# Attention rows transposed three tiles behind their scores, weighted values one step later, with more row buffers

## The chip, the cores and the metric

The kernel runs on one core of one Trainium2 chip. The metric is device time in microseconds, from one launch to the end of the program, as the median of several runs. TensorE does the matrix products and the transposes, VectorE (DVE in the profile) and ScalarE (ACT) the work on rows, GpSimd (POOL) a few copies and masks, and SyncE (SP) issues most transfers.

## The reference

One decoder layer on 1024 tokens of width 1024, in float32. After an RMS norm one projection feeds three kinds of heads; their results go through one output projection, and a squared-ReLU MLP (width 4096) follows. The change touches the two kinds of attention:

```python
# stick-breaking, 6 heads of 64, strictly causal
z = einsum('bhqd,bhsd->bhqs', qi, k) * scale
log_1mb = where(mask, log_sigmoid(-z), 0.0)
tail = cumsum(log_1mb, axis=3, reverse=True) - log_1mb
A = where(mask, exp(log_sigmoid(z) + tail), 0.0)
o = einsum('bhqs,bhsd->bhqd', A, v)
# forgetting, 6 heads of 64, causal; c is the running sum of log forget gates
s = einsum('bhqd,bhsd->bhqs', qi, k) * scale + (c[q] - c[s])
o = einsum('bhqs,bhsd->bhqd', softmax(where(mask, s, -1e30)), v)
```

Two further units, `hg0` and `hg1`, are HGRN2 (a gated linear recurrence) and are computed by levels and chunks.

## The kernel before, in words

The mixing part is eight units, run in the order m0, hg0, m1, m2, m3, hg1, m4, m5. A unit m*p* is one stick-breaking head (h = 0) and one forgetting head (h = 1). Each unit has two parts. Its projection (`proj_attn`, or `proj_hg`) multiplies the normed input by the unit's weights; every product is made of three matmuls of rounded high and low parts (`mm3`, L167 to L169, output `pj`). Its core (`attn`) is the attention itself. The core of one unit is interleaved in the source with the projection of the next (`place`, with `SPAN` and `POW`); the core of the last unit, m5, is interleaved with the first part of the output projection (`wo_tile`, output `po`, the same three lines). The framework then schedules every engine's instructions from this source order with a planner of its own, and each engine runs its list strictly in that order. So between the score matmuls of a head and its transposes TensorE has projection matmuls to do, as far as they have not been used up: the text calls them filler.

A core works on 16 row tiles of 128 queries, in steps. A step s does three things:

- `qprep` (every second tile): queries transposed (`qtp`, L366), scaled into `qj` by ScalarE (L368) and VectorE (L369).
- `qtile`, tile s: the scores `z` on TensorE (L391, L392, mask L394), up to two pieces of at most 512 keys. For h = 0 VectorE scales them into a row tile `sbz` (L400), ScalarE takes exp and ln (L401, L402, tile `sbe`), VectorE scans (L404, tile `sbr`) and subtracts (L407), ScalarE takes exp (L408). For h = 1 VectorE subtracts the gates and takes the maximum (L413, tile `fxa`), ScalarE takes exp with a row sum (L425), VectorE the reciprocal, and ScalarE scales (L434).
- `back`, tile s - SKEW: TensorE transposes the finished row tile in blocks of 128 by 128 (`atp`, L446), and ScalarE (L450) or VectorE (L452) copies the result out of PSUM into `at`. Once a group of two tiles of both heads is through, `av` multiplies by the values (L465), in the same step, and the result is split into high and low parts.

Tiles have fixed numbers of buffers (`BUFS`): row tiles `zs` (these are `sbz`, `fxa`, and also the level tiles `hx` of HGRN2 and the squares of both norms), function tiles `e`, scan tiles `r`, and `at`. In PSUM the scores and the query transposes share three buffers, the row transposes have two, and `av` shares one with the key transposes `ktp` (L314).

## Time and profile before

| what | value |
|---|---|
| median of 3 runs | 1349.1 us (1346.22 to 1351.35) |
| the profiled execution's own time | 1347.27 us |
| its span, first to last instruction | 1345.5 us |
| mean granted TensorE clock | 0.977 |
| 0 to 70 us (norm, first projection) | PE busy 52.06 us, DVE 49.78, ACT 40.49 |
| 70 to 660 us (the eight cores) | PE busy 560.66 us, DVE 440.87, ACT 389.40 |
| 660 to 735 us (output projection, second norm) | PE busy 68.12 us, DVE 64.10, ACT 41.50 |
| 735 to 1345.5 us (MLP) | PE busy 602.18 us, DVE 431.03, ACT 255.63 |

PE is TensorE's matmuls and PEld its weight loads. A matmul's row runs to its modelled end, and the next one starts earlier: dense matmuls overlap in the table, so the busy time of PE overstates its work. What a matmul costs in a dense stretch is read from the distance of two starts. Each weighted-value product is two matmuls in the trace.

### The profile page before, as it was taken

How to read it: one execution, taken by the hardware profiler on the slowest of the kernel's cores; microseconds unless marked ns; L12 is line 12 of the kernel's file. 1: busy time of each engine (PE TensorE's matmuls, PEld its weight loads, DVE VectorE, ACT ScalarE, POOL GpSimd, SP SyncE). 2: the span in 40 equal slices, each digit the busy share in tenths (PEclk: the TensorE clock that was granted, in tenths of full speed). 3: DMA queues.
4: the chain of work that ended last, by engine and by line, in shares of the span. 5: the costliest groups of instructions: out<-in, count | busy, mean ns of one | idle time of the engine just before them, and what ended most of it. 6: DMA issues, size and time to landing. Idle time of an engine off the chain costs nothing.

```text
span 1345.5 us, 19762 instructions
## 1 busy us (share of the span) xinstructions
PE 1283.0 (95%) x7200; PEld 1063.1 (79%) x7200; DVE 985.8 (73%) x1844; ACT 727.0 (54%) x1557; POOL 90.3 (7%) x138
## 2 busy tenths in 40 slices
PE   4999889989999999999798999999999999999998
PEld 4978789878688988767586888888887788888887
DVE  6758798766768788867579766666666897786965
ACT  5658445877878457776446454455454433333330
POOL 7000021002110130000000000000000000000000
PEclk9999999989899989999898999999999999999999
DMA  8200220301203025524443434444445972634322
GB/s 231 46 17 18 62 58 18 92 16 54 49 17 79 17 57 177 183 64 125 149 152 107 164 126 164 164 130 145 149 163 175 391 247 94 218 96 153 113 79 94
DMA packets 129737, 156.57 MB, mean 116 GB/s; under 512 B 46684, under 2 KB 73308, under 8 KB 129640
## 3 DMA queue, kind: packets, MB, share of 16 engines
q1 hardware_dynamic: 104496, 109.14, 26.8%
q10 hardware_dynamic: 25144, 46.17, 9.6%
q8 instruction: 57, 0.93, 0.3%
q14 instruction: 40, 0.33, 0.1%
HBM read 108.07 MB, written 47.21 MB: 115 GB/s over the span
## 4 chain that ended last, share of the span: by engine, by line
PE 80%; DVE 10%; ACT 4%; DMA 4%; issue 2%; SPq 0%; ACTq 0%; DVEq 0%
PE pj L167 6%; PE pj L169 6%; PE pj L168 6%; PE av L465 3%; PE atp L446 2%; PE pc L1021 2%; PE pc L1022 2%; PE pc L1023 2%; PE pd L1021 2%; PE pd L1022 2%; PE pd L1023 2%; PE pc L1202 2%; PE pc L1200 2%; PE pc L1201 2%; PE pa L1023 2%; PE pa L1021 2%
## 5 line engine op out<-in xcount | busy, mean ns | idle before, releaser
L167 PE MATMUL pj<-whi,hTh 128*128 128x384 f32 (+2 forms) x512 | 172.2, 339 | 0.0
L169 PE MATMUL pj<-whi,hTl 128*128 128x384 f32 (+2 forms) x512 | 171.9, 336 | 0.0
L168 PE MATMUL pj<-wlo,hTh 128*128 128x384 f32 (+2 forms) x512 | 170.6, 334 | 0.5 <-DVE wlo L127 0.4
L124 ACT CAST fah<-ya 128x1024 fp32r<-128x1024 f32 x56 | 58.7, 1048 | 166.8 <-PE pd L1201 50.0
L167 PEld LDWEIGHTS pj<-whi,hTh 128*128 128x128 f32 x512 | 98.7, 193 | 3.6 <-issue 1.1
L168 PEld LDWEIGHTS pj<-wlo,hTh 128*128 128x128 f32 x512 | 98.5, 192 | 3.5 <-issue 1.3
L169 PEld LDWEIGHTS pj<-whi,hTl 128*128 128x128 f32 x512 | 98.4, 192 | 2.3 <-issue 1.5
L127 DVE TENSOR_TENSOR fal<-ya,fah 128x1024 fp32r<-128x1024 f32 x56 | 68.3, 1219 | 23.2 <-ACT fah L124 23.1
L465 PE MATMUL av<-at,vst 128*64 128x256 f32 x480 | 71.3, 384 | 6.3 <-DVE at L452 3.0
L450 ACT COPY at<-atp 128x128 f32<-128x128 f32 (+3 forms) x120 | 55.5, 475 | 20.5 <-PE atp L446 19.5
L465 PEld LDWEIGHTS av<-at,vst 128*64 128x64 f32 x480 | 38.3, 144 | 33.2 <-issue 8.4
L127 DVE TENSOR_TENSOR fbl<-w2raw,fbh 128x1024 fp32r<-128x1024 f32 x48 | 58.0, 1215 | 1.6 <-ACT fbh L124 1.6
L408 ACT ACTIVATE sbz<-sbz 128x128 f32<-128x128 f32 (+3 forms) x72 | 37.7, 525 | 37.8 <-DVE sbz L407 37.2
L400 DVE TENSOR_SCALAR sbz<-z,qnr 128x128 f32<-128x128 f32 (+3 forms) x72 | 42.5, 611 | 20.6 <-PE z L394 12.9
L167 PE MATMUL po<-woh,mTh 128*128 128x512 f32 x128 | 52.1, 409 | 4.5 <-DMA mTh<-mix_m 3.6
L124 ACT CAST fbh<-w2raw 128x1024 fp32r<-128x1024 f32 x48 | 50.0, 1047 | 8.1 <-DMA w2raw<-in_w_ff_dram 5.1
L391 PE MATMUL z<-kst,qj 128*128 128x512 f32 (+3 forms) x144 | 51.3, 384 | 2.8 <-ACT qj L368 2.8
L1201 PE MATMUL pa<-fbl,fah 128*128 128x512 f32 x128 | 50.3, 395 | 1.9 <-DVE fbl L127 1.8
L1200 PE MATMUL pd<-fbh,fah 128*128 128x512 f32 x128 | 49.5, 399 | 2.3 <-ACT fbh L124 2.3
L168 PE MATMUL po<-wol,mTh 128*128 128x512 f32 x128 | 51.1, 399 | 0.0
L392 PE MATMUL z<-kst,qj 128*128 128x512 f32 (+3 forms) x144 | 49.6, 370 | 1.5 <-DVE qj L369 1.4
L169 PE MATMUL po<-woh,mTl 128*128 128x512 f32 x128 | 50.6, 398 | 0.0
(349 smaller groups left out, 3626.3 us busy)
## 6 DMA issues: line engine op xcount, KB each, us to landing
w1raw<-in_w_ff_dram SPq DMA_DIRECT2D x32, 512.0 KB, 4.6
w2raw<-in_w_ff_dram SPq DMA_DIRECT2D x16, 1024.0 KB, 7.1
ya<-yd_s SPq DMA_DIRECT2D x32, 512.0 KB, 3.6
yd_s<-y ACTq DMA_DIRECT2D x48, 256.0 KB, 4.6
ya<-yd_a SPq DMA_DIRECT2D x24, 512.0 KB, 3.7
wraw<-in_w_in_dram SPq DMA_DIRECT2D x48, 192.0 KB, 3.0
mix_m<-ot ACTq DMA_DIRECT2D x10, 512.0 KB, 3.7
wraw<-in_w_in_dram SPq DMA_DIRECT2D x16, 256.0 KB, 3.6
```

The lines of the kernel that those rows point to most:

```text
L124: S.copy(hi, raw)
L127: lo_eng.tensor_tensor(out=lo, in0=raw, in1=hi, op=ALU.subtract)
L167: PE.matmul(o, lhsT=lh, rhs=rh, start=start, stop=False)
L168: PE.matmul(o, lhsT=lh, rhs=rl, start=False, stop=False)
L169: PE.matmul(o, lhsT=ll, rhs=rh, start=False, stop=stop)
L450: S.copy(dst, tv)
L465: PE.matmul(o[h * HD:(h + 1) * HD, c0:], lhsT=st["v"][j // 4][:, j % 4, h, :], rhs=at[h][j // 4][:, j % 4, c0:], start=(j == 0), stop=(j = ...
L1021: PE.matmul(o, lhsT=wh[:, k], rhs=bh[:, k], start=start and k == 0, stop=False, **kw)
L1022: PE.matmul(o, lhsT=wh[:, k], rhs=bl[:, k], start=False, stop=False, **kw)
L1023: PE.matmul(o, lhsT=wl[:, k], rhs=bh[:, k], start=False, stop=k == 3, **kw)
L1200: PE.matmul(o, lhsT=lh[:, ts], rhs=rh, start=start and q == q0, stop=False, **kw)
L1201: PE.matmul(o, lhsT=lh[:, ts], rhs=rl, start=False, stop=False, **kw)
```

## The change

The transposes come three tiles behind the scores, not two. `av` is no longer called at the end of `back`, but at the next step, behind that step's scores and ahead of its transposes; the last group's follows its transposes at once. There are three more row tiles `zs` (8), one more function tile `e` (3) and one more scan tile `r` (3). Room for them (6144 of the 10240 bytes a partition) comes from the scratch area for dynamic DMAs; a padding tile of the MLP's second half grows by the same 6144 bytes, so that later tiles keep their places.

```diff
-    "BUFS": {... "zs": 5, "e": 2, "r": 2, ...},
+    "BUFS": {... "zs": 8, "e": 3, "r": 3, ...},
-    "SKEW": [2, 2, 2, 2, 2, 2],
+    "SKEW": [3, 3, 3, 3, 3, 3],
...
                 if cur["n", g] == 2:
-                    av(g)
+                    ready.append(g)
...
         steps = []
+        ready = []
...
                 if s < len(tiles):
                     qtile(*tiles[s])
+                while ready:
+                    av(ready.pop())
                 if s >= SKEW:
                     back(*tiles[s - SKEW])
+                if s == len(tiles) + SKEW - 1:
+                    av(ready.pop())
...
-    PLACES = {"f_m": {... "pad": (1, [P, 136 + 2048])},
+    PLACES = {"f_m": {... "pad": (1, [P, 136 + 3584])},
...
-    nc = _bacc.Bacc("TRN2", ..., dynamic_dma_scratch_size=8192)
+    nc = _bacc.Bacc("TRN2", ..., dynamic_dma_scratch_size=2048)
```

The planner makes a new order of the whole mixing part. Three places of TensorE's list show it. The first is the end of m0's core, where the last stick-breaking row tiles (`sbz`) are transposed; before:

```order
L391 MATMUL z<-kst_426,qj 128x512
L392 MATMUL z<-kst_426,qj 128x512
L446 MATMUL atp<-ident,sbz 128x128 x4
L167 MATMUL pj<-whi,hTh 128x384 x2
L446 MATMUL atp<-ident,sbz 128x128 x4
```

and now:

```order
L446 MATMUL atp<-ident,sbz 128x128 x4
L167 MATMUL pj<-whi,hTh 128x384 x2
L391 MATMUL z<-kst_426,qj 128x512
L392 MATMUL z<-kst_426,qj 128x512
L446 MATMUL atp<-ident,sbz 128x128 x4
```

Two projection matmuls stood between the two sets of four transposes; now the last scores stand there too, and 22 projection matmuls stand ahead of the first set. Behind this place 22 projection matmuls came before the first transposes of a forgetting tile (`fxa`); now 46 do.

The second place is the end of m1's core, at the last projection matmul of m2's first half; before:

```order
L169 MATMUL pj<-whi,hTl 128x384
L391 MATMUL z<-kst_2225,qj 128x384
L391 MATMUL z<-kst_1961,qj 128x512
L392 MATMUL z<-kst_2225,qj 128x384
L394 LDWEIGHTS identb
L394 MATMUL z<-m_strict,identb 128x128
L392 MATMUL z<-kst_1961,qj 128x512
L391 MATMUL z<-kst_2225,qj 128x512
L392 MATMUL z<-kst_2225,qj 128x512
```

and now:

```order
L169 MATMUL pj<-whi,hTl 128x384
L446 MATMUL atp<-ident,fxa 128x128 x4
L465 MATMUL av<-at,vst 64x256
L446 MATMUL atp<-ident,sbz 128x128
L391 MATMUL z<-kst_1962,qj 128x512
L392 MATMUL z<-kst_1962,qj 128x512
L366 MATMUL qtp<-ident,qd 128x128 x2
L465 MATMUL av<-at,vst 64x256 x5
L465 MATMUL av<-at,vst 64x128 x2
L446 MATMUL atp<-ident,sbz 128x128 x6
L391 MATMUL z<-kst_2225,qj 128x384
L391 MATMUL z<-kst_1961,qj 128x512
```

The filler ends earlier: the scores of the last stick-breaking tiles (`kst_2225`, `kst_1961`) came at once behind the last projection matmul, and now a group of transposes and a whole `av` stand between. Until the next projection matmul there were 26 transposes, and now there are 52.

The third place is the end of m5's core, the last of all; before:

```order
L465 MATMUL av<-at,vst 64x256 x9
L465 MATMUL av<-at,vst 64x128 x2
L446 MATMUL atp<-ident,sbz 128x128 x8
L391 MATMUL z<-kst_6213,qj 128x512
L392 MATMUL z<-kst_6213,qj 128x512
L446 MATMUL atp<-ident,sbz 128x128 x4
L465 MATMUL av<-at,vst 64x256
L446 MATMUL atp<-ident,fxa 128x128 x15
L465 MATMUL av<-at,vst 64x256 x13
```

and now:

```order
L465 MATMUL av<-at,vst 64x256 x9
L391 MATMUL z<-kst_6209,qj 128x512
L392 MATMUL z<-kst_6209,qj 128x512
L465 MATMUL av<-at,vst 64x128 x2
L446 MATMUL atp<-ident,sbz 128x128 x4
L169 MATMUL po<-woh,mTl 128x512
L446 MATMUL atp<-ident,sbz 128x128 x8
L446 MATMUL atp<-ident,fxa 128x128 x7
L465 MATMUL av<-at,vst 64x256
L446 MATMUL atp<-ident,fxa 128x128 x8
L465 MATMUL av<-at,vst 64x256 x13
```

The last score matmuls (`z` of 512 keys) come eight transposes and two value products sooner, and the last filler (`po`) stands behind them, not ahead.

## Prediction

> **What bounds the kernel now.** I read the page's chain first, then busy times by stretch, then who TensorE waits for, then the timeline around the waits.

> ```profile
> span 1345.5 us, 19762 instructions
> PE 80%; DVE 10%; ACT 4%; DMA 4%; issue 2%; SPq 0%; ACTq 0%; DVEq 0%
> ```

> ```profile
> 70.00:660.00 590.00, 560.66 (x3998) 469.32 (x3997) 440.87 (x997) 389.40 (x981) 64.32 (x84) 0.97 0.24 67
> 735.00:1345.50 610.50, 602.18 (x2608) 490.68 (x2606) 431.03 (x568) 255.63 (x354) 0.00 (x0) 0.99 0.47 159
> ```

> The chain is four fifths TensorE. The second fence has length, then busy PE, PEld, DVE, ACT, POOL, clock, DMA share and GB/s. All that the change moves lies in 70 to 660 us; of the MLP behind 735 us it moves nothing but addresses. Both stretches look full, but a row of PE hides idling, since rows overlap. The work of one matmul is the distance of two starts:

> ```profile
> 635.80 0.39 PE L391 MATMUL z<-kst,qj 128*128 128x512 f32 x1
> 636.03 0.40 PE L392 MATMUL z<-kst,qj 128*128 128x512 f32 x1
> ...
> 636.43 2.59 PE L465 MATMUL av<-at,vst 128*64 128x256 f32 x22
> ```

> That gives 0.23 us for 512 columns of scores. The value products start at 636.43 and the next work at 638.95:

> ```profile
> 638.95 1.09 PE L446 MATMUL atp<-ident,sbz 128*128 128x128 f32 x8
> 639.80 0.48 PE L391 MATMUL z<-kst,qj 128*128 128x512 f32 x1
> ```

> So 22 of them are 2.52 us (0.115 each) and a transpose is 0.85 / 8 = 0.11 us. With these I went through the core stage and looked for stretches in which TensorE has attention work alone, no projection matmuls between. Five of them lose more than a microsecond:

> ```profile
> 139.10:152.30 13.20, 8.50 (x46) 6.53 (x44) 11.16 (x30) 5.50 (x15) 0.00 (x0) 1.00 0.47 104
> 266.10:286.90 20.80, 16.04 (x89) 10.02 (x88) 17.91 (x35) 18.20 (x42) 1.62 (x3) 0.85 0.08 26
> 349.70:363.20 13.50, 10.51 (x69) 7.96 (x68) 9.51 (x26) 10.44 (x24) 1.01 (x2) 0.85 0.12 41
> 547.80:554.40 6.60, 4.82 (x29) 3.24 (x27) 5.33 (x13) 6.54 (x18) 0.61 (x1) 1.00 0.60 199
> 586.70:602.80 16.10, 13.14 (x91) 8.54 (x89) 12.30 (x29) 11.31 (x28) 1.66 (x3) 1.00 0.20 65
> 634.50:657.10 22.60, 16.67 (x95) 10.76 (x93) 9.78 (x24) 10.11 (x22) 0.00 (x0) 0.77 0.27 82
> ```

> Rows two to six are those five; the first is the end of m0, which has filler. At the prices above their own matmuls are 10.9, 7.9, 3.8, 10.5 and 10.9 us (the first: 26 transposes 2.9, 26 value products 3.0, scores 3.9, other transposes 1.1). They last 79.6 us for 44.0 us of work: 35.6 us lost. In the second and fourth row ScalarE is busy 18.20 of 20.80 and 6.54 of 6.60 us: without filler, the softmax chain through ScalarE and VectorE sets the pace, not TensorE.

> **The change, part by part.** No operation is added or removed: the work on each engine is the same, and TensorE's transposes, value products and copies only stand elsewhere. Three terms follow.

> *The end of m0.* TensorE waits there for three things:

> ```profile
> PE atp L446 <- ACT sbz L408: 1.8, 1, 1.8
> PE atp L446 <- ACT fxa L434: 1.3, 1, 1.3
> PE av L465 <- DVE at L452: 1.1, 1, 1.1
> ```

> The transposes now stand behind 22 and 46 projection matmuls (0.17 us each, by the next two starts, so 24 more are 4.1 us of cover against a wait of 1.3).

> ```profile
> 153.44 0.34 PE L169 MATMUL pj<-whi,hTl 128*128 128x384 f32 x1
> 153.62 0.34 PE L167 MATMUL pj<-whi,hTh 128*128 128x384 f32 x1
> ```

> Both transposes' waits, 3.1 us, should go; the wait for a copy ahead of `av` keeps 10 filler matmuls instead of 12 and stays. Bounds: 0, if VectorE (11.16 of 13.20 us busy) is what is late, and -4.2. I take -3.

> *The stretches without filler.* By the order of the changed program they hold 52, 19, 29 and 23 transposes, with 18.4, 3.9, 12.2 and 5.9 us of TensorE work; those of before hold 26, 22, 9, 20 and 30. The first is nearly twice as long, because the filler is used up earlier; the one before m5's last group is gone; the last is shorter, because a filler matmul stands in it. Their price has two bounds from the rows above. Per microsecond of TensorE work the five lost 35.6 / 44.0 = 0.81, which on 40.4 us gives 32.7, or -2.9. Per transposed block they lost 35.6 / 107 = 0.33, which on 123 blocks gives 41.0, or +5.4. I take the ScalarE count between them: in the first stretch, by the two orders, it has 70 instructions instead of 42; at 18.20 / 42 = 0.43 us that is 30.3: 12 us lost on 18.4 us of TensorE work, where 9.9 were lost. With 42 instructions in the third (18.2, lost 6), 18 in the second (7.8, lost 4) and the tail as it is (11.7) that is 33.5, or -2, which lies within what a mean over unlike instructions hides. I take 0.

> *The tail of m5.* From the last scores (639.80) to the first output matmul there were 17.3 us:

> ```profile
> 657.13 0.50 PE L167 MATMUL po<-woh,mTh 128*128 128x512 f32 x1
> ```

> It is a chain: maximum, two exps, reciprocal, two scalings, transposes, copies, values. The last scores now come ahead of two value products and eight transposes, 1.1 us of work, which then fall inside the chain. Bounds: 0, if VectorE's own queue is late, and -1.3 with the filler matmul of 0.23; I take -1.

> *More buffers.* VectorE waits for a free row tile:

> ```profile
> L400 DVE TENSOR_SCALAR sbz<-z,qnr 128x128 f32<-128x128 f32 (+3 forms) x72 | 42.5, 611 | 20.6 <-PE z L394 12.9 <-PE atp L446 7.2
> L413 DVE CUSTOM_DVE_ANT_0 fxa<-z,cb 128x128 f32<-128x128 f32 (+3 forms) x72 | 38.9, 550 | 10.6 <-PE z L394 8.0 <-PE atp L446 1.4 <-PE z L392 0.6
> ```

> The 7.2 and 1.4 us behind `atp` are row tiles still held by transposes; three tiles in flight use one or two of the new buffers themselves. These waits are VectorE's; what they cost is already in the stretches. HGRN2 and the norms use the same tags:

> ```profile
> PE hz L671 <- DVE hxq L666: 3.4, 3, 2.5
> ...
> PE n2tp L156 <- DVE n2sq L153: 1.1, 1, 1.1
> ```

> There TensorE waits for VectorE's work, not for a buffer of these kinds as far as the rows say; 0 to -1, taken as 0. The smaller DMA scratch is free: every transfer goes over queues that the page calls hardware_dynamic or instruction, and no POOL issue is listed.

> ```profile
> q1 hardware_dynamic: 104496, 109.14, 26.8%
> q10 hardware_dynamic: 25144, 46.17, 9.6%
> ```

> *New waits.* `av` stands ahead of the next tile's transposes, so these and their copies wait for up to 30 value products (3.5 us of work that is done in any case), and ScalarE and VectorE wait behind a late copy. With five `at` buffers, of which two groups of four can be asked for at once, a copy can wait for that `av` alone: 0 to +1 us each; taken as 0, since transposes follow `av` in TensorE's own list.

> Sum: -3 + 0 - 1 = -4 us against the profiled execution's 1347.3 us, so 1343. That run lies 0.14% under the median of 1349.1 us; on the median it is 1345.

> [...] In the first stretch TensorE ran at half clock, though it was never long idle:

> ```profile
> PE av L465 <- DVE kst L320: 2.2, 2, 1.3
> ...
> PE z L392 <- DVE qj L369: 0.8, 2, 0.6
> ```

> ```profile
> 284.10:290.90 6.80, 5.82 (x19) 4.63 (x18) 2.93 (x9) 6.28 (x17) 0.61 (x1) 0.50 0.10 28
> ```

> The longest wait in that stretch is 1.3 us, and 6.8 us at clock 0.50 followed. So I give the longer stretch another such piece in the slow case: at most half of 6.8, 3.4 us. [...]

> **The rivals.**

> *Row tiles were what was short (faster).* Then ScalarE enters a stretch one tile ahead.

> ```profile
> L450 ACT COPY at<-atp 128x512 f32<-128x512 f32 (+3 forms) x9 | 4.3, 509 | 0.1
> ...
> L408 ACT ACTIVATE sbz<-sbz 128x512 f32<-128x512 f32 (+1 forms) x4 | 2.4, 606 | 0.2
> ```

> A tile of 1024 keys costs it three functions on two pieces, 3.6 us at 0.6 us each, and two copies, 1.0 us. Two long stretches save 4.6 us each, 9.2; with -3 and -1 the sum is -13, 1336. For it speaks the 7.2 us above; against it, that ScalarE was at 18.20 of 20.80 in the very stretch that doubles, so it has no lead to carry in. [...]
> *The long stretch goes by blocks (slower).* At the end of m1 52 blocks at 0.33 us and the others cost +5.4, the clock 3.4, and the gains at m0 and in the tail don't come since VectorE is late there: +8.8, 1358. It decides from a length of the first stretch of about 38 us, instead of the 30 to 31 of my forecast. For it: in the first stretch of before 20.80 us went for 26 blocks, 0.80 a block, which on 52 is 41.6. Against it: that stretch also had three query preparations and two sets of keys, and these do not double twice.

> *The change does nothing at all:* the three score buffers in PSUM cap how far scores run ahead, whatever the skew. Then 1349. It differs from the forecast by 4 us and stands in the same class.

> **How the numbers follow.** About 0.5% (7 us) is what a measurement of this kernel tells from no change. Forecast together with the change that does nothing: 0.46, nearly all within that, a small part faster. Row tiles: 0.33. Blocks: 0.21, a little of it within. Faster 0.36, same 0.44, slower 0.20. The likeliest time is 1345, with 1340 to 1350 as its own range; the range of all three reaches from 1334, just past the fast rival, to 1357, near the slow one.

> **What would show it.** Right: no wait of `atp` at m0's end; one stretch of 30 to 33 us without projection matmuls at the end of m1, with ScalarE busy nine tenths of it; the stretch before m5's last group gone; the time from 735 us to the end the same. Wrong: a first stretch of 26 us or less (row tiles), or near 40 with two pieces at half clock (blocks), or a loss in the HGRN2 cores, which I left at nothing.

## Result: 10.8 us faster, and where the time went in the profile after

The median fell from 1349.1 to 1338.3 us (1337.3 to 1340.2). The ratio to the kernel before is 0.9925, with a 95% interval of 0.9909 to 0.9941. I had forecast 1345 and within 0.5%; the measurement is 0.75% faster. The time lies in the wide range of 1334 to 1357, which I had stretched for the rivals, but outside the 1340 to 1350 that I gave to my own forecast.

The profiled execution took 1337.9 us. Its span, its chain by engine, and the two stretches (length, then busy PE, PEld, DVE, ACT, POOL, clock, DMA share, GB/s):

```profile
span 1336.1 us, 19720 instructions
PE 77%; DVE 10%; ACT 6%; DMA 4%; issue 2%; POOL 1%; SPq 0%; ACTq 0%; POOLq 0%; DVEq 0%
```

```profile
70.00:660.00 590.00, 561.63 (x4035) 468.39 (x4033) 439.52 (x1014) 391.85 (x992) 68.94 (x84) 0.98 0.24 69
735.00:1336.00 601.00, 592.05 (x2569) 482.29 (x2568) 425.79 (x559) 251.55 (x347) 0.00 (x0) 1.00 0.46 159
```

Busy times hardly move. I take the same measure as in the prediction: at any point, the time passed less the TensorE work done by then, at the distances of two starts. That is what has been lost so far. At the end of m5's third group it was 86.2 us before and 86.6 now: through five and three quarters of six attention cores nothing was gained on balance. Over m5's last group 11.2 us were lost before and 3.2 now. From the second norm to the end the time went from 679.2 to 677.4 us. So +0.4, -8.0 and -1.8 make the 9.4 us between the two spans.

The group ends are the rows in which ScalarE casts the result of `av`. Before, the third and the last group of m5:

```profile
639.05 0.37 ACT L124 CAST mTh<-av 128x256 fp32r<-128x256 f32 x1 [0.92 <-PE av L465]
...
657.24 0.37 ACT L124 CAST mTh<-av 128x256 fp32r<-128x256 f32 x1 [5.86 <-PE av L465]
```

and after:

```profile
640.70 0.35 ACT L124 CAST mTh<-av 128x256 fp32r<-128x256 f32 x1
...
649.65 0.37 ACT L124 CAST mTh<-av 128x256 fp32r<-128x256 f32 x1 [3.54 <-PE av L465]
```

Between them 18.2 us passed before and 8.95 now; 1.2 us of this is work now done ahead of the first row. The timeline shows two causes. Before, the last tile's maximum (`fxmn`), its transposes and the last value products:

```profile
643.80 0.20 DVE L422 TENSOR_SCALAR fxmn<-fxm 128x1 f32<-128x1 f32 x1
...
648.79 1.97 PE L446 MATMUL atp<-ident,fxa 128*128 128x128 f32 x8 [0.94 <-ACT fxa L434]
...
651.44 5.77 PE L465 MATMUL av<-at,vst 128*64 128x256 f32 x30 [0.67 <-ACT at L450]
```

and after, from the last scores to the first output matmul:

```profile
638.08 0.50 PE L391 MATMUL z<-kst,qj 128*128 128x512 f32 x1
...
640.58 0.20 DVE L422 TENSOR_SCALAR fxmn<-fxm 128x1 f32<-128x1 f32 x1
...
644.34 1.13 PE L446 MATMUL atp<-ident,fxa 128*128 128x128 f32 x8 [0.74 <-ACT fxa L434]
...
646.16 3.45 PE L465 MATMUL av<-at,vst 128*64 128x256 f32 x30 [0.69 <-ACT at L450]
...
649.54 0.50 PE L167 MATMUL po<-woh,mTh 128*128 128x512 f32 x1
```

First, the maximum came 4.0 us behind the last scores and comes 2.5 us behind them now; the last transposes 9.0 and now 6.3. Second, the same 30 matmuls of the value products took 5.77 us and take 3.45. The windows say why, the first two of before and the third of after:

```profile
642.49:645.90 3.41, 0.65 (x2) 0.19 (x2) 1.58 (x7) 1.79 (x4) 0.00 (x0) 1.00 1.06 358
645.90:656.10 10.20, 8.38 (x37) 5.55 (x39) 0.91 (x3) 4.20 (x9) 0.00 (x0) 0.50 0.18 52
```

```profile
642.60:646.00 3.40, 2.13 (x14) 1.22 (x12) 0.82 (x3) 3.00 (x6) 0.00 (x0) 1.00 0.80 246
```

TensorE was busy 0.65 of 3.41 us while it waited for the last softmax, and 10.2 us at clock 0.50 followed. After, the thinnest such window is 2.13 us full and the clock stays at 1.00.

The stretches without filler elsewhere, in the order of the prediction, and the half-clock piece in the first:

```profile
260.90:293.60 32.70, 26.40 (x156) 17.51 (x154) 24.93 (x62) 30.44 (x78) 3.04 (x6) 0.91 0.09 33
358.20:364.50 6.30, 5.27 (x41) 4.12 (x39) 4.02 (x15) 6.25 (x15) 1.01 (x2) 1.00 0.00 1
547.10:564.90 17.80, 15.08 (x103) 9.80 (x101) 16.25 (x34) 16.46 (x42) 2.64 (x3) 1.00 0.50 168
...
639.80:649.50 9.70, 7.48 (x56) 4.73 (x54) 3.43 (x10) 5.91 (x13) 0.00 (x0) 1.00 0.53 164
287.60:294.40 6.80, 6.06 (x21) 4.25 (x22) 5.32 (x18) 6.72 (x22) 0.72 (x2) 0.50 0.01 2
```

The first is the long one that I had forecast: ScalarE is busy 30.44 of 32.70 us, and 14.3 us are lost on 18.4 us of TensorE work. The second and third lose 2.4 and 5.6. That makes 22.3, where the four stretches of before ahead of m5's last group lost 23.9; what is lost elsewhere takes the 1.6 us back, and 0.4 more.

### The profile page after: what moved, and what is told of

Its sections match the earlier page's. It is cut to its first block, busy times and chain, and to the rows that moved or that the text cites. A ratio compares the mean times of both kernels' runs of the same rounds, so it can differ in the third digit from the quotient of the medians.

```text
span 1336.1 us, 19720 instructions
## 1 busy us (share of the span) xinstructions
PE 1274.0 (95%) x7200; PEld 1054.1 (79%) x7200; DVE 978.2 (73%) x1844; ACT 725.8 (54%) x1557; POOL 94.5 (7%) x138
## 3 DMA queue, kind: packets, MB, share of 16 engines
q1 hardware_dynamic: 104496, 109.14, 26.8%
q10 hardware_dynamic: 25144, 46.17, 9.7%
## 4 chain that ended last, share of the span: by engine, by line
PE 77%; DVE 10%; ACT 6%; DMA 4%; issue 2%; POOL 1%; SPq 0%; ACTq 0%; POOLq 0%; DVEq 0%
PE pj L167 6%; PE pj L168 5%; PE pj L169 5%; PE av L465 3%; PE pc L1027 2%; PE pc L1026 2%; PE pc L1028 2%; PE pd L1026 2%; PE pd L1027 2%; PE pd L1028 2%; PE pc L1207 2%; PE pc L1205 2%; PE pc L1206 2%; PE pa L1026 2%; PE pa L1028 2%
## 5 line engine op out<-in xcount | busy, mean ns | idle before, releaser
L167 PE MATMUL pj<-whi,hTh 128*128 128x384 f32 (+2 forms) x512 | 171.1, 337 | 1.7 <-DVE vst L296 1.7
L169 PE MATMUL pj<-whi,hTl 128*128 128x384 f32 (+2 forms) x512 | 170.3, 333 | 0.0
L167 PEld LDWEIGHTS pj<-whi,hTh 128*128 128x128 f32 x512 | 98.2, 192 | 4.6 <-issue 1.5
L169 PEld LDWEIGHTS pj<-whi,hTl 128*128 128x128 f32 x512 | 98.3, 192 | 1.6 <-issue 0.9
L465 PE MATMUL av<-at,vst 128*64 128x256 f32 x480 | 67.6, 367 | 3.2 <-DVE at L452 2.3
L450 ACT COPY at<-atp 128x128 f32<-128x128 f32 (+3 forms) x120 | 55.5, 476 | 21.0 <-PE atp L446 18.2
L465 PEld LDWEIGHTS av<-at,vst 128*64 128x64 f32 x480 | 36.5, 136 | 27.8 <-issue 7.2
L400 DVE TENSOR_SCALAR sbz<-z,qnr 128x128 f32<-128x128 f32 (+3 forms) x72 | 42.3, 610 | 20.5 <-PE z L394 18.5
L167 PE MATMUL po<-woh,mTh 128*128 128x512 f32 x128 | 51.9, 408 | 3.7 <-DMA mTh<-mix_m 2.8
L425 ACT ACTIVATE fxa<-fxa,fxmn 128x512 f32<-128x512 f32 (+2 forms) x72 | 43.7, 609 | 19.1 <-DVE fxmn L422 12.9
L391 PE MATMUL z<-kst,qj 128*128 128x512 f32 (+3 forms) x144 | 48.9, 373 | 2.3 <-ACT qj L368 1.6
L169 PE MATMUL po<-woh,mTl 128*128 128x512 f32 x128 | 51.0, 402 | 0.0
L392 PE MATMUL z<-kst,qj 128*128 128x512 f32 (+3 forms) x144 | 49.1, 372 | 1.4 <-DVE qj L369 1.3
```

What stands on the lines that cost most here:

```text
L167: PE.matmul(o, lhsT=lh, rhs=rh, start=start, stop=False)
L169: PE.matmul(o, lhsT=ll, rhs=rh, start=False, stop=stop)
L450: S.copy(dst, tv)
L465: PE.matmul(o[h * HD:(h + 1) * HD, c0:], lhsT=st["v"][j // 4][:, j % 4, h, :], rhs=at[h][j // 4][:, j % 4, c0:], start=(j == 0), stop=(j = ...
```

## Experiments

The theory, formed from the two traces: the gain lies in the tail of m5, because the changed order leaves output matmuls (`po`, filler) among the last tiles' work and puts the last softmax chain earlier, so TensorE stays at full clock. Rival 1: row tiles were short everywhere. Rival 2: the later transposes and the later `av` save time in every core. Every kernel was timed beside the kernel before on the same chip (medians of before 1349.3, 1347.3, 1348.6 and 1348.1 in the four sessions).

| kernel | median us | ratio to before (95%) | `po` ahead of / behind the last scores | half clock in the tail, us | lost ahead of the tail / in it, us | second norm to end, us |
|---|---|---|---|---|---|---|
| before | 1349.1 | | 0 / 0 | 10.2 | 86.2 / 11.2 | 679.2 |
| after | 1338.3 | 0.9925 (0.9909 to 0.9941) | 3 / 1 | 0 | 86.6 / 3.2 | 677.4 |
| e1 buffers alone | 1343.8 | 0.9963 (0.9950 to 0.9976) | 9 / 0 | 10.2 | 88.5 / 9.8 | 675.2 |
| e2 order alone | 1344.0 | 0.9968 (0.9956 to 0.9980) | 0 / 0 | 6.8 | 87.6 / 8.1 | 677.6 |
| e7 order in m5 alone | 1345.1 | 0.9962 (0.9946 to 0.9978) | 5 / 4 | 3.4 | 87.2 / 6.2 | 675.2 |
| e8 order in all but m5 | 1345.8 | 0.9978 (0.9966 to 0.9989) | 0 / 0 | 13.7 | 86.2 / 11.3 | 677.4 |
| e5 `av` at once | 1342.2 | 0.9953 (0.9939 to 0.9967) | 5 / 4 | 3.4 | 88.7 / 5.5 | 678.7 |
| e6 two tiles behind | 1337.2 | 0.9921 (0.9901 to 0.9941) | 5 / 4 | 3.4 | 84.8 / 5.3 | 678.7 |
| f1 tail without filler | 1342.8 | 0.9953 (0.9936 to 0.9970) | 0 / 0 | 6.8 | 88.8 / 8.0 | 675.6 |
| f3 more filler | 1335.7 | 0.9911 (0.9895 to 0.9926) | 13 / 9 | 0 | 85.3 / 2.3 | 675.9 |
| h1 m4's filler later | 1341.5 | 0.9954 (0.9936 to 0.9972) | 0 / 4 | 6.8 | 89.7 / 7.4 | 678.7 |

The last three columns come from the one profiled execution of each, which is not always near the median (e7's took 1339.3 us, h1's 1346.5); `po` are counted in the program's order, "ahead" from the scores of the last tile but one. The tail's loss goes with the half clock in it: 2.3 and 3.2 us without, 5.3 to 6.2 with 3.4, 7.4 to 8.1 with 6.8, 9.8 to 11.3 with 10.2 or 13.7. That alone doesn't say which causes which, since a long wait is itself a loss; the last part of this section separates them.

**Which part does it.** Buffers alone:

```diff
-"zs": 5, "e": 2, "r": 2     (kernel before)
+"zs": 8, "e": 3, "r": 3     (and the pad and scratch sizes of the change)
```

> The kernel before with the new buffers alone (8 row tiles, 3 function tiles, 3 scan tiles, the smaller DMA scratch); transposes two tiles behind, av at once. By the program's order nine output matmuls (po) now stand just ahead of the last scores of m5, none did before. Theory (the tail of m5 was what cost, since TensorE had nothing but the last tiles' softmax there and fell to half clock): the last scores to the first output matmul behind the last av take 10 to 13 us instead of 17.3, no half-clock piece of 10 us in it, whole time 1339 to 1343. Rival 1 (row tiles were what was short, everywhere): 1338 to 1340, with the gain spread over the long stretches. Rival 2 (the later transposes and av are the gain): 1347 to 1351.

Measured 1343.8 us. By the profile the mixing part became 1.0 us longer (the second norm starts at 667.3 us, not 666.3); the gain is behind it. VectorE's waits on row tiles did go:

```profile
L400 DVE TENSOR_SCALAR sbz<-z,qnr 128x128 f32<-128x128 f32 (+3 forms) x72 | 42.3, 612 | 31.1 <-PE z L394 28.1 <-PE z L392 2.8
```

The 7.2 us behind `atp` are gone, and the wait for scores grew from 12.9 to 28.1. So rival 1 falls. The theory's tail (10 to 13 us, no half clock) was missed too: the nine `po` stand ahead of the last scores, and behind them nothing fills: 15.8 us and the whole half-clock piece.

The order without the buffers:

```diff
-"zs": 8, "e": 3, "r": 3     (kernel after; and its pad and scratch sizes)
+"zs": 5, "e": 2, "r": 2
```

> The change without its buffers: transposes three tiles behind, av one step later, but 5 row tiles, 2 function tiles, 2 scan tiles and the old DMA scratch. By the program's order the tail of m5 has no output matmul in it, as before. Theory (tail): 17 us from the last scores to the next output matmul, a half-clock piece there, whole time 1346 to 1351. Rival 1 (row tiles were short): 1347 to 1352, with longer waits of VectorE for row tiles, since three tiles in flight need more of them. Rival 2 (the order of transposes and av is the gain): 1338 to 1342.

Measured 1344.0 us: under the numbers of the theory and of rival 1, over those of rival 2. The tail lost 8.1 us with 6.8 at half clock; the last scores stand four transposes earlier than in before. This part alone gives under half. So neither the buffers nor the order alone shorten the tail as both do; of before, e1, e2 and after, only after has a `po` behind the last scores.

The order in m5 alone, and in all but m5 (both with the buffers):

```diff
-"SKEW": [3, 3, 3, 3, 3, 3]
+"SKEW": [2, 2, 2, 2, 2, 3]     (e7; e8: [3, 3, 3, 3, 3, 2])
...
-                    ready.append(g)
+                    ready.append(g) if pr == 5 else av(g)     (e8: if pr != 5)
...
-                if s == len(tiles) + SKEW - 1:
+                if ready and s == len(tiles) + SKEW - 1:
```

> The new buffers, and the later transposes and the later av in m5 alone; m0 to m4 keep two tiles and av at once. By the program's order output matmuls stand in the tail of m5 (five ahead of the last scores, four behind them). Theory (tail): 1338 to 1342, the gain between the end of m5's third group and the first output matmul, 6 to 9 us of it. Rival 1 (row tiles everywhere): 1338 to 1341, but with the gain in the stretches of m1 to m4. Rival 2 (later transposes and av in all cores): a sixth to a third of 10.8 us, so 1345 to 1348.

> The whole change with its buffers, except that m5 keeps transposes two tiles behind and av at once. By the program's order the tail of m5 has no output matmul in it, as before. Theory (tail): the gain goes; 17 us from the last scores to the next output matmul, half clock there, whole time 1345 to 1350. Rival 1 (row tiles): 1337 to 1340. Rival 2 (later transposes and av in all cores): two thirds to five sixths of 10.8 us stay, 1340 to 1342.

e8 is as the theory says: the tail is as before and the mixing part ends at 666.4 us, as before (666.3). Its last value products stand nearly wholly at half clock (0.50 from 643.2 to 656.9 us):

```profile
650.89 6.41 PE L465 MATMUL av<-at,vst 128*64 128x256 f32 x30 [0.68 <-ACT at L450]
```

That speaks against rival 2: five cores with the new order and the new buffers gave nothing up to there. The median of e8 is still 0.22% under that of before; in its profile the gain lies behind the second norm (677.4 us, not 679.2). e7 takes 5.0 us off the tail's loss (expected 6 to 9), and its mixing part is 3.9 us shorter. But its seven executions fall into 1339 to 1342 and 1345 to 1346, and the median lies in the upper group: the theory's 1338 to 1342 was missed.

Each of the two halves of the order taken out:

```diff
-                    ready.append(g)
+                    av(g)                       (e5, without the two calls of av in the steps)
-"SKEW": [3, 3, 3, 3, 3, 3]
+"SKEW": [2, 2, 2, 2, 2, 2]                      (e6)
```

> The kernel after with av called at once, as before; transposes three tiles behind and the new buffers stay. By the program's order four output matmuls stand behind the last scores of m5 and five ahead of them. Theory (what the tail loses goes by the filler left in it, whichever part of the change leaves it): the tail loses 3 to 6 us instead of 11.2, whole time 1338 to 1343. Rival (the later av is what shortens the tail): tail 8 us or more lost, 1344 to 1349.

> The kernel after with transposes two tiles behind, as before; the later av and the new buffers stay. By the program's order four output matmuls stand behind the last scores of m5 and five ahead of them. Theory (filler left in the tail): the tail loses 3 to 6 us, whole time 1338 to 1343. Rival (the third tile of lead is what shortens the tail): 8 us or more lost, 1344 to 1349.

Both tails are within the theory, and so is e5's time; e6's 1337.2 us is 0.8 under its 1338 to 1343. e6 is as fast as the whole change: the third tile of lead isn't needed beside the later `av` and the buffers. Of its gain, 5.9 us are in the tail and 1.4 ahead of it.

**Does filler in the tail do it?** Two kernels change one number of after, the power by which the output projection's first matmuls are spread over m5:

```diff
-"POW": [0.7, 1.1, 1.3, 1.3, 0.9, 1.2, 1, 1.5]
+"POW": [0.7, 1.1, 1.3, 1.3, 0.9, 1.2, 1, 2.0]     (f1; f3: 1.0)
```

> The kernel after with one number changed: the output projection's first matmuls (filler of m5) are placed earlier (power 2.0 instead of 1.5), so that none is left in the tail of m5; transposes, late av and buffers as in the change. Theory (filler in the tail keeps TensorE at full clock): a half-clock piece of 7 to 14 us in the tail, 8 to 11 us lost behind m5's third group instead of 3.2, whole time 1342 to 1348. Rival (the later transposes, the late av or the buffers shorten the tail by themselves): no half clock, 1337 to 1340.

> The kernel after with the same number the other way (power 1.0): nine output matmuls now stand behind the last scores of m5 and thirteen just ahead of them, instead of one and three. Theory: the tail stays at full clock and loses 2 to 3.5 us; since after lost 3.2 there already, 1336 to 1339. Rival 1 (filler in the tail delays the last transposes, as av does): 1339 to 1342. Rival 2 (what is taken from the stretch ahead of m5's third group opens a new loss there): 1340 to 1345, with a half-clock piece between 590 and 640 us.

f1 keeps skew, `av` and buffers, and loses about 4 us of the gain (ratio 0.9953 instead of 0.9925); its mixing part ends at 665.8 us instead of 658.7, 4.8 of it by the tail. The intervals of f1 and after just overlap; those of f1 and f3 do not. The half clock is back, and with it the last transposes and products are long, though the transposes come only 6.6 us behind the last scores:

```profile
648.20:655.00 6.80, 5.52 (x27) 3.57 (x28) 0.00 (x0) 2.23 (x5) 0.00 (x0) 0.50 0.15 53
```

```profile
642.28 0.49 PE L391 MATMUL z<-kst,qj 128*128 128x512 f32 x1
...
648.84 1.97 PE L446 MATMUL atp<-ident,fxa 128*128 128x128 f32 x8 [0.60 <-ACT at L450]
...
656.57 0.50 PE L167 MATMUL po<-woh,mTh 128*128 128x512 f32 x1
```

f3 goes the other way. Its last scores, maximum, transposes and products:

```profile
634.63 0.50 PE L391 MATMUL z<-kst,qj 128*128 128x512 f32 x1
...
636.24 0.22 DVE L422 TENSOR_SCALAR fxmn<-fxm 128x1 f32<-128x1 f32 x1
...
642.09 1.09 PE L446 MATMUL atp<-ident,fxa 128*128 128x128 f32 x8
...
643.91 3.45 PE L465 MATMUL av<-at,vst 128*64 128x256 f32 x30 [0.73 <-ACT at L450]
```

The maximum follows the scores by 1.6 us, the tail loses 2.3. f3 is 1335.7 us; its interval overlaps that of after, so it is not shown to be better.

The same idea for m4's stretch, on top of f3:

```diff
-"POW": [0.7, 1.1, 1.3, 1.3, 0.9, 1.2, 1, 1.0]
+"POW": [0.7, 1.1, 1.3, 1.3, 0.9, 0.9, 1, 1.0]
```

> The kernel with the fed tail (after, with the output projection's power 1.0) and one more number: m4's projection is spread later (power 0.9 instead of 1.2), so that by the program's order the stretch at m4's second group holds 11 transposes and 5.2 us of TensorE work instead of 29 and 12.2, the rest of m4's core having filler. Theory (what a stretch loses goes by how long TensorE has attention work alone): its loss falls from 5.4 us to 2 to 3, whole time 1331 to 1335. Rival (the loss only moves, because the filler is taken from elsewhere): 1335 to 1338.

The stretch became 6.7 us and lost 1.5, less than expected. But the loss moved, and further than the rival had it: 7.7 us instead of 2.7 up to the end of m4's first group, with a half-clock piece at 508.7 us, and the tail's order changed as well (7.4 lost). 1341.5 us.

**Is the half clock a cost or a mark of waiting?** Three kernels put value products whose results are not used into the tail of before, and leave the rest of the mixing part as it is. They write the half of the bank that `av` does not use (`spare` is that bank, taken ahead of `av`):

```diff
+            if name == LASTNAME and g == 3 and (h, par) in ((0, 1), (1, 0)):
+                ...
+                src = cur["at", h, g][1][:, 0, :P * (2 - h)]
+                for j in range(4 if h == 0 else 5):     (g4; g3: 9 and 9)
+                    PE.matmul(cur["spare"][:HD, 256:256 + P * (2 - h)], lhsT=src[:, :HD], rhs=src, start=True, stop=True)
```

> The kernel before with 20 extra value products, whose results are not used, in the tail of m5 alone: 12 between the last stick-breaking transposes and the first forgetting ones, 8 between the two sets of forgetting transposes; every other instruction of TensorE stands where it stood. They are 4.6 us more work (20 by 2 matmuls by 0.115 us), in a tail of 17.3 us that had 6 us of waits and 10.2 us at half clock. Theory (the half clock is a cause: TensorE idles, the clock falls, and the transposes and values behind take up to twice as long): no half-clock piece, or 3.4 us of one, in the tail; from the last scores to the first output matmul 13 to 15 us in spite of the added work, whole time 1344 to 1347. Rival 1 (the half clock is only a mark of waiting, VectorE's queue sets the tail): 17 to 18 us and 1348 to 1351. Rival 2 (the clock does not go by how much TensorE has to do): the half-clock piece stays and the added work costs up to 4.6 us, 1349 to 1354.

g1, with ten products at each of the two places, read both `at` chunks and gave 1352.3 us (ratio 1.0033, 1.0022 to 1.0045), as rival 2. But the clock had gone up: only 3.4 us at half clock, the last products 3.46 us. The added work was mispriced and stood in the way: its first 24 matmuls, 2.8 us at my price, ran from 644.38 to 651.23 us, ahead of the transposes.

> Again the kernel before with value products whose results are not used in the tail of m5 alone, but fewer and with operands that are there earlier: 9 of 256 columns behind the last stick-breaking transposes (they need only copies that land about 642.6 us) and 9 of 128 columns between the two sets of forgetting transposes. Nothing else moves up to the end of the mixing part. They are 3.1 us of work (18 matmuls of 0.115 us and 18 of 0.057), in waits of 3.9 us and 1.3 us. Theory (the clock of a window of 3.4 us follows how much of the window before it TensorE was busy, and the half clock is a cost of its own): at most one half-clock piece of 3.4 us in the tail, the last value products take 3.5 us instead of 5.77, from the last scores to the first output matmul 13.3 to 15.5 us instead of 17.3. Rival (the half clock only marks a wait, the softmax chain sets the tail): 17 us or more, since the chain is the same. The whole time goes with it: 1344 to 1347 or 1347 to 1351.

1346.1 us (0.9978, 0.9967 to 0.9989), with a tail of 17.9 us: the theory's total, the rival's tail. The 18 added matmuls held up the transposes to 648.01 us:

```profile
642.50 5.58 PE L458 MATMUL av<-at 128*64 128x256 f32 x18 [0.49 <-DVE at L452]
648.01 0.98 PE L446 MATMUL atp<-ident,fxa 128*128 128x128 f32 x7
...
653.49 3.45 PE L471 MATMUL av<-at,vst 128*64 128x256 f32 x30 [0.73 <-ACT at L450]
```

> As the last kernel with unused value products in the tail of the kernel before, with 4 of 256 columns instead of 9 in the first wait and 5 of 128 instead of 9 in the second. The last run showed that such a product of one head alone takes 0.43 us (two matmuls of 0.215), and one of 128 columns 0.22: so 1.7 us at full clock (3.4 at half) in a wait of 3.6, and 1.1 in one of 1.8; they no longer delay the forgetting transposes. Theory (the half clock has a price of its own, about 4 us in this tail: last value products 3.45 instead of 5.77 us, transposes 1.0 and 1.1 instead of 1.75 and 1.97): from the last scores to the first output matmul 13 to 15 us instead of 17.3, whole time 1343 to 1346. Rival 1 (the half clock only marks a wait): 17 us, 1347 to 1350. Rival 2 (the added work is too little to lift the clock): a half-clock piece of 6.8 us or more stays, 16 to 18 us.

This one doesn't hold up the transposes: 1344.5 us (0.9976, 0.9967 to 0.9986), no half clock in the tail.

```profile
640.30 0.48 PE L391 MATMUL z<-kst,qj 128*128 128x512 f32 x1
...
644.60 0.20 DVE L422 TENSOR_SCALAR fxmn<-fxm 128x1 f32<-128x1 f32 x1
...
649.79 1.09 PE L446 MATMUL atp<-ident,fxa 128*128 128x128 f32 x8
...
651.61 3.45 PE L471 MATMUL av<-at,vst 128*64 128x256 f32 x30 [0.73 <-ACT at L450]
...
654.99 0.50 PE L167 MATMUL po<-woh,mTh 128*128 128x512 f32 x1
```

The softmax chain is no earlier than before (the maximum 4.3 us behind the scores, the last transposes 9.5; before 4.0 and 9.0), and yet from scores to output matmul 14.7 us pass instead of 17.3, with more work in it. So the half clock is a cost. From the last transposes to the output matmul it was 8.3 us before, and is 5.2 in g4 and 5.2 in after: 3.1 of the 5.9 us by which after is shorter there (17.3 to 11.5). The other 2.7 belong to the earlier chain: the last transposes come 6.3 us behind the scores instead of 9.0.

f1 tells the two apart. Without filler its transposes come 6.6 us behind the scores, nearly as early as in after, but from them to the output matmul 7.7 us pass. So in this tail the filler keeps the clock up (no half clock in after, 6.8 us in f1), and the earlier chain is not its doing. VectorE's list shows where that comes from. Before, VectorE works without a gap from 639.65 us to the last maximum at 643.80, and both halves of the last `fxa`, three copies and the split of the third group's result stand in that list. After, of the long instructions only one half and one copy stand between the last scores and the maximum; the other half came ahead of the scores. The last 2.1 of the 8.0 us are that the last scores start 2.6 us ahead of the third group's end, not 0.7 behind it, less the 1.2 us of work done there.

## Why the prediction was right or wrong

**The tail of m5** is the step that failed: -1 us, bounds 0 to -1.3, and -8.0 measured. I had counted only the 1.1 us of work that moves into the chain. I had the row with clock 0.77 for that stretch and took the clock as given; without its piece at half clock the transposes and products behind the wait take 3.1 us less (g4). And I called the rest "as it is" without following VectorE's list to the last maximum, where another 2.7 us lay, and without asking how far ahead the last scores would come (2.1). That the time still lies in the stated range is owed to the room that I left for the rivals, not to this term.

**The stretches without filler** were sized nearly right. I forecast 30 to 31 us for the first with ScalarE nine tenths busy (32.7, and 30.44 busy), 12 lost in it (14.3), 6 in the third (5.6), 4 in the second (2.4), and that the one before m5's last group goes. Without the tail the sum is -1.6 us, inside my bounds, where -2 was forecast. Some of that is luck: the first and the second stretch miss in opposite directions, and ScalarE had 78 instructions of 0.39 us in the first, not 70 of 0.43.

**The end of m0**: both waits of `atp` for ScalarE are gone, as forecast, but only 0.8 us came of the 3 (6.8 lost over m0's last group, now 6.0). The clock took back 1.5 of the rest. A half-clock piece of 3.4 us starts at 151.0 us, where before had none, and the projection matmuls in it start 0.32 us apart instead of 0.17. In f3 and e8, which have the same order up to there and no such piece, the group loses 2.3 us less than before. What is late next is a copy of VectorE, which I had left as it was at 1.1 us:

```profile
PE av L465 <- DVE at L452: 2.3, 1, 2.3
...
PE atp L446 <- DVE at L452: 0.5, 1, 0.5
```

**More buffers** at 0: right for the buffers alone (e1: the mixing part 1.0 us longer), but not beside the new order, where leaving them out costs 5.9 us of the mixing part (it ends at 664.6 us in e2, at 658.7 in after). I had added up the parts as if each acted by itself. **New waits** at 0: the stretches show no cost of the later `av`, and by e6 and e5 it is the better half of the order.

**The HGRN2 cores**, which I left at nothing: from the end of m0's core to the end of m1's first group after loses 1.1 us more than before, and f1, f3 and e8, with the same order up to there, 3.3 to 3.5 more (g1, g3 and g4, with before's order, stay within 0.4 of before). Of this stretch 6.8 us are at half clock in before and in after, and 10.2 to 13.7 in those three. This sign of being wrong did show; whether it comes from the order or from where the clock's windows fall was not tested.

**From 735 us on the same**: counted from the same matmul, it was 0.4 us less there; of the 1.8 us gained behind the second norm the other 1.4 lie ahead of that point. From the second norm to the end the fourteen profiles take 675.2 to 679.4 us for nearly the same order, and they part at two places alone, near 715 us and between 1032 and 1067 us, where each has half-clock pieces. The seven with 3.4 us at half clock near 715 us take 675.2 to 677.6 us (after: 3.4 at 714.2), the seven with 6.8 or 10.2 us 678.3 to 679.4 (before: 10.2 at 717.6).

**The rivals.** "Row tiles" named 1336, nearest to the result, for a reason that did not hold: the long stretch lost 14.3 us and not less, and the buffers alone did not shorten the mixing part. Of "blocks" the long stretch got under a third (14.3 lost, against 12 by my forecast and 20 by blocks), and no second half-clock piece. None of the three had the case that decided: a tail that gets filler.

**The clock.** The longer stretch had one piece at half clock, 6.8 us from 287.6 (before had one of 6.8 there and one of 3.4 besides), so the slow case's extra piece did not come. What the piece came from is in the last section.

## What to carry to other kernels

Look at the end of the last unit by itself: there the filler ran out in before, and a long wait counted twice, once as idling (TensorE busy 0.65 of 3.41 us) and once in the clock of the work behind it (10.2 us at 0.50, 3.1 us of the gain). Keep a few independent matmuls for behind the last scores, not ahead of them, and look for what stands in VectorE's queue ahead of the last reduction. Price a row of the clock column like any other stall, and when several parts of a change are tested alone, read the stage as well as the total, since the clock elsewhere moved too (3.4 to 10.2 us at half clock near 715 us).

## What the runs showed of the hardware

**The grid had no fixed place in the program.** Before, g1, g3 and g4 have one order up to m5's tail, and their grids lie 0.80, 2.38, 0.42 and 1.46 us behind the first instruction; a piece at 273 us is in the traces of before and g3 and not in those of g1 and g4. That is likely also the spread of 7 to 10 us between executions of e6, e7 and h1 (in h1 the mean clock was 0.978 in the three over 1346 us and 0.987 in the two under 1340), of which only one each was profiled; that was not tested. The tail of after hangs on it less than that of before: laid anywhere between the last scores and the end of m5, a window of 3.41 us is covered for at least 0.58 there (0.66 in f3), and in before for as little as 0.18.

**A value product cost half where its twin of the other head stood beside it**: 0.115 us a matmul of 256 columns in `av`, where the heads alternate between the two 64-row halves of the result, and 0.215 in g3 and g4, where one half is used alone (g4's first eight take 1.94 us). The starts of after's last `av` show the pairs: two matmuls 0.007 us apart, the next two 0.21 us later. I had priced the added products at 0.115, which is why g1 and g3 cost more than their waits had room for.
